# Expert outputs through rows in DRAM, and gate and up weights in runs of 4 KB, in a one-core encoder layer

## The chip, the cores and the metric

The kernel runs on one core of a Trainium2 chip. The metric is device time of one execution in microseconds (us). The core has TensorE (PE, with its weight loads PEld), VectorE (DVE), ScalarE (ACT), GpSimd (POOL) and SyncE (SP), which share an on-chip memory of 128 partitions (SBUF) and an accumulator memory (PSUM, 8 banks). 16 DMA engines move data between SBUF and DRAM; SP and POOL issue the DMAs here.

## The reference

One encoder layer on 512 tokens of width 1024, in float32: a mixer (a state space scan and a gated delta net), a cross attention over 256 memory rows, and a mixture of experts. Only the last part is touched. Each token goes to 2 of 32 experts, whose weights are 1024x256 (gate), 1024x256 (up) and 256x1024 (down):

```python
g_logits = (t @ wg).astype(F32) + bg.astype(F32)
p_top, g_idx = lax.top_k(jax.nn.softmax(g_logits, axis=-1), 1)
...
e_val, e_idx = lax.top_k(e_sel, MOE_TOPK)
e_w = jax.nn.softmax(e_val, axis=-1) * p_top
...
h = (jax.nn.silu(jnp.einsum('td,edf->tef', t, w_gate[sl]))
     * jnp.einsum('td,edf->tef', t, w_up[sl]))
h = h * combine[:, grp][..., None]
out = out + jnp.einsum('tef,efd->td', h, w_down[sl])
```

The result is added to the layer's input of this part and normalised. The weights of the 32 experts are 100.7 MB, 3.1 MB an expert.

## The kernel before, in words

The mixer and the cross attention fill the first 640 us. Then the routing (`moe_route`) works out for each expert up to 64 slots of tokens. Experts are worked on in 16 pairs of two, one on each half of the 128 rows of a tile. For pair q:

- `pair_tokens` (L1316): POOL gathers the slots' tokens from `t_scr` in DRAM by an indirect DMA (rows with a number past 511 are left out; 1,024 token slots in all, so 64 of the 128 rows of a pair on average) into one of two tiles `xg`; PE transposes them in 8 matmuls (L1327), ACT copies them to `xt`.
- `pair_up` (L1333): 16 matmuls of 512 columns (L1340) against the gate and up weights, then the gated product `hs` (ACT L1343, DVE L1344).
- `pair_down` (L1347): two transposes of `hs` (L1355), 8 matmuls of 512 columns (L1364) against the down weights into two banks; ACT and DVE write the result as a high and a low part `y`.
- `scatter` (L1370): a 0/1 matrix `st` of slots and tokens takes the slots back to the tokens' rows: for each of the 4 blocks of 128 tokens and 2 halves of the columns two matmuls (L1377; 16 a pair) and one DVE add into the residual `xr` (L1378).

The weights come in units of 1 MB, four of gate and up weights and two of down weights for a pair, 96 in all (`load_unit`, L1301). They have 19 places in SBUF that go round: 13 of gate and up weights, 6 of down weights, so some 3 pairs. SP issues each load when the matmuls that read the place before are done; a DMA also waits for the one eight before it in SP's queue. 18 units are loaded before the first pair starts, one more as soon as the first gather has landed, and 77 behind it. A gate or up unit is a tile `[P, 4, 2, 256]` in which gate and up columns take turns, so its two DMAs write runs of 256 numbers (1 KB), though the rows in DRAM hang together for 4 KB.

The order on each engine is fixed when the program is built, by a scheduler that follows estimated times; PE works on the matmuls of pair q+1, the down weights of pair q and the scatter of pair q-1 in turns. Banks 0 and 1 of PSUM serve both `pair_up` and `pair_down`. At the end (`moe_final`, L1380) each block is normalised and written out by SP.

Of the kernel before, what the change touches and what calls it, by code (L numbers as in the profile page):

```python
# [9 lines left out]
F32 = mybir.dt.float32  # L10
# [21 lines left out]
P = 128  # L32
# [11 lines left out]
def weave(*streams):  # L44
    """run generators side by side, (generator, number of its steps) each, evenly"""
    live = [[g, n, 0] for g, n in streams]
    while live:
        s = min(live, key=lambda t: (t[2] + 0.5) / t[1])
        s[2] += 1
        if next(s[0], s) is s:  # L50
            live.remove(s)
# [6 lines left out]
class Enc:  # L58
# [6 lines left out]
    def set_banks(self, **kw):  # L65
        """the PSUM banks of each stream of work: streams that run side by side do not share banks"""
        self.banks.update(kw)
        self.turn.update({n: 0 for n in kw})
# [7 lines left out]
    # ---------------------------------------------------------------- consts  # L76
    def consts(self):
# [13 lines left out]
        self.ltb = cp.tile([P, P], BF16, name="ltb")          # [t', t] = t' < t  # L91
# [14 lines left out]
    # ------------------------------------------------- normalise and transpose  # L106
    def rms_T(self, pool, tiles, gain, hi, lo, tag, between=None, junk=None):
        """tiles: list of [128 tok, D] token blocks -> hi/lo [128, 8, ntok] (feature p*8+k)."""
# [25 lines left out]
    # weight columns [128, 8, w]: staged, split into fp32r hi and lo parts  # L134
    def wsplit(self, src, w, lo_eng=None, tag="w"):
        """src: DRAM AP [128, 8, w]."""
# [9 lines left out]
    def mm3(self, ps, pairs, first=True, last=True):  # L146
        """pairs: list of ((lhsT_hi, lhsT_lo), (rhs_hi, rhs_lo))"""
# [6 lines left out]
    # ---------------------------------------------------------------- stage A  # L154
# [26 lines left out]
    def proj(self, c0):  # L181
        """feature-major projection of 128 columns from c0 -> PSUM [128, 512]"""
# [18 lines left out]
    # ---------------------------------------------------------------- S5  # L201
    def acc_exp(self, pool, out, x, n, tag):
        """out = exp(x) to float32 accuracy, x [128, n]"""
# [17 lines left out]
    def cmul(self, eng, pool, ore, oim, are, aim, bre, bim, shape, tag):  # L221
        """(ore + i oim) = a * b, elementwise on APs of the given shape"""
# [9 lines left out]
    def s5_params(self):  # L232
# [3 lines left out]
        with tc.tile_pool(name="s5t", bufs=1, side="right") as tq:  # L236
# [6 lines left out]
            with tc.tile_pool(name="s5i", bufs=1, side="right") as tp:  # L243
# [27 lines left out]
                # C^T: [lane, (re, -im), g, c']  # L271
# [5 lines left out]
                # step, a = exp(lam*step)  # L277
# [19 lines left out]
                # powers a^0 .. a^8  # L297
# [11 lines left out]
                # aR: conjugate of (fwd a^m, bwd a^(7-m));  aF: fwd a^(7-m), bwd a^m  # L309
# [6 lines left out]
                # a^8 with real part twice, (-im, im)  # L316
# [6 lines left out]
                # f = (a - 1)/lam  # L323
# [15 lines left out]
                # Bbar = f*b (a padded group at the end), B1 = a*Bbar  # L339
# [5 lines left out]
            with tc.tile_pool(name="s5l", bufs=1, side="right") as tl:  # L345
                # diag(d) per group
# [5 lines left out]
                for gg in range(8):  # L352
# [4 lines left out]
                    # P = aF * B1  # L357
# [3 lines left out]
                    # Ca_re, -Ca_im  # L361
# [5 lines left out]
                    # BcT: [(m c), cg, ri, (dir p)]  # L367
# [7 lines left out]
                    # local kernels  # L375
# [117 lines left out]
    # ---------------------------------------------------------------- GDN  # L493
# [23 lines left out]
    def gates(self):  # L517
# [6 lines left out]
        with tc.tile_pool(name="gt_", bufs=1) as tp:  # L524
# [5 lines left out]
            # rows 32i..: the projection's part from the feature blocks i and i + 4; the sums in token order  # L530
# [19 lines left out]
            # beta = 1/(1+exp(-x))  # L550
# [3 lines left out]
            # g = -exp(a_log) * softplus(a + dt)  # L554
# [17 lines left out]
            # chunk cumulative sums and totals  # L572
# [14 lines left out]
            # per-step scalars: rows of the forward chunk n, rows of the backward chunk 7-n  # L587
            # csr: -beta_f*egc_f | -egc_b ; csv: 1 | beta_b ; cso: egc_f | egc_b
# [13 lines left out]
    def gdn_alloc(self):  # L602
# [4 lines left out]
        self.kn = gp.tile([P, 4, 4, P], F32, name="kn")        # blk, h, d  # L607
        self.vc = gp.tile([P, 8, 4, P], F32, name="vc")        # step, h, dv
# [4 lines left out]
    def gdn_in(self, blocks, tp):  # L613
        """projection, convolution, silu, norms, token-major and feature-major operands.
        The transposes of a block come after the projections of the next ones."""
# [1111 lines left out]
```

## Time and profile before

| | us |
|---|---|
| runs | 959.79, 962.05, 950.4; median 959.79 |
| span of the profiled execution | 956.5 |
| experts, from the first gather (652.9) to the end | 303.6 |
| PE busy in the span | 842.3 (88%) |
| DVE, ACT, POOL busy | 548.9, 374.0, 274.6 |
| DMA | 173.25 MB, of it 161.30 MB read from and 15.17 MB written to DRAM |

The page gives the span of the profiled execution and no other time of it; the median of the runs lies 3.3 us above the span. A busy PE is not PE at its peak, as matmuls are pipelined. DMA shares can pass 1.0 because packets overlap in an engine.

### The profile page before, as it was taken

The numbers are of one execution on the slowest core, as the hardware profiler recorded it, in microseconds if no ns is written. First come the engines' busy times: TensorE is split into PE (matmuls) and PEld (weight loads), VectorE is DVE, ScalarE is ACT, GpSimd is POOL, SyncE is SP. The second block draws the span as 40 slices with busy tenths as digits, with TensorE's granted clock in tenths as the row PEclk, the third lists the DMA queues.
The fourth block names the chain that finished last, engine by engine and source line by source line (L and its number), as shares of the span: only waits on it lengthen the run. The fifth ranks groups of instructions, "written<-read, shape, count | busy, mean of one in ns | idle before, by whom it ended". The sixth has DMA issues, their size and how long they took to land.

```text
span 956.5 us, 14240 instructions
## 1 busy us (share of the span) xinstructions
PE 842.3 (88%) x5247; PEld 574.6 (60%) x5248; DVE 548.9 (57%) x1195; ACT 374.0 (39%) x815; POOL 274.6 (29%) x234
## 2 busy tenths in 40 slices
PE   5898888887855889898999999975999999999995
PEld 4676566666855757685788789972344344343432
DVE  5599999698999973235533634134144344344345
ACT  6544554675224328235524644322322122121224
POOL 3154597435542411003451332322100000000003
PEclk9997899999896898589999999996999999999998
DMA  8774223212531164317646325984999999999502
GB/s 203 135 92 130 79 87 94 73 56 78 163 108 58 49 120 116 64 45 209 216 144 198 111 66 189 360 288 134 342 379 364 365 377 362 366 375 363 199 1 90
DMA packets 173977, 173.25 MB, mean 181 GB/s; under 512 B 37584, under 2 KB 157392, under 8 KB 170064
## 3 DMA queue, kind: packets, MB, share of 16 engines
q1 hardware_dynamic: 171600, 168.11, 57.0%
q0 software_dynamic: 2304, 4.20, 1.3%
q8 instruction: 42, 0.69, 0.3%
q14 instruction: 31, 0.25, 0.1%
HBM read 161.30 MB, written 15.17 MB: 185 GB/s over the span
## 4 chain that ended last, share of the span: by engine, by line
PE 51%; DMA 4%; DVE 3%; ACT 3%; SPq 2%; issue 1%; POOL 0%; DVEq 0%; ACTq 0%; POOLq 0%
PE bank L1340 13%; PE bank L1364 7%; PE bank L1377 7%; PE bank L152 5%; PE bank L151 5%; PE bank L150 5%; PE bank L1327 2%; DMA tz<-w_scr 2%; DMA kvs<-kv_scr 1%; PE bank L850 1%; PE bank L833 1%; PE bank L802 1%; PE bank L1355 1%; PE bank L801 1%; SPq L430 1%
## 5 line engine op out<-in xcount | busy, mean ns | idle before, releaser
L1378 DVE TENSOR_TENSOR xr<-xr,bank 128x512 f32<-128x512 f32 x120 | 76.3, 683 | 117.8 <-PE bank L1377 117.6
L1340 PE MATMUL bank<-mw,xt 128*64 128x512 f32 x400 | 118.5, 609 | 0.0
L143 POOL TENSOR_TENSOR wlo<-wst,whi 128x1024 fp32r<-128x1024 f32 x24 | 58.3, 2433 | 56.5 <-ACT whi L142 39.2
L150 PE MATMUL bank<-htl,whi 128*128 128x512 f32 x160 | 68.0, 426 | 7.3 <-ACT whi L142 4.1
L1377 PE MATMUL bank<-y,st 128*128 128x512 f32 x240 | 70.2, 416 | 4.4 <-ACT y L1366 3.4
L1320 POOL DMA_INDIRECT xg<-t_scr,tidx x16 | 16.4, 1022 | 191.7 <-PE bank L1327 160.9
L1340 PEld LDWEIGHTS bank<-mw,xt 128*64 128x64 f32 x400 | 33.9, 139 | 59.6 <-issue 53.7
L152 PE MATMUL bank<-hth,wlo 128*128 128x512 f32 x160 | 66.5, 416 | 0.0
L151 PE MATMUL bank<-hth,whi 128*128 128x512 f32 x160 | 66.4, 415 | 0.0
L1343 ACT ACTIVATE hs<-bank,tw 128x256 f32<-128x256 f32 x16 | 7.6, 473 | 147.5 <-PE bank L1340 147.5
L1377 PEld LDWEIGHTS bank<-y,st 128*128 128x128 f32 x240 | 41.2, 189 | 38.7 <-issue 17.0
L973 POOL TENSOR_TENSOR wlo<-wst,whi 128x1024 fp32r<-128x1024 f32 x16 | 38.4, 2403 | 82.5 <-ACT whi L972 82.5
L142 ACT ACTIVATE whi<-wst 128x1024 fp32r<-128x1024 f32 x36 | 38.1, 1059 | 26.6 <-DMA wst<-in_w_in_dram 11.3
L641 DVE SCALAR_TENSOR_TENSOR cv<-xp,taps,cv 128x512 f32<-128x512 f32 x48 | 46.6, 972 | 0.4
L1364 PE MATMUL bank<-mw,hT 128*64 128x512 f32 x128 | 46.3, 601 | 0.0
L152 PE MATMUL bank<-mth,wlo 128*128 128x256 f32 x128 | 40.2, 314 | 6.7 <-POOL wlo L143 6.7
L150 PE MATMUL bank<-mtl,whi 128*128 128x256 f32 x128 | 40.4, 316 | 3.5 <-ACT zt L683 3.5
L1330 ACT ACTIVATE xt<-bank,gm 128x128 f32<-128x128 f32 x128 | 34.9, 386 | 20.6 <-PE bank L1327 20.3
L150 PEld LDWEIGHTS bank<-htl,whi 128*128 128x128 f32 x160 | 32.4, 203 | 15.3 <-ACT whi L142 4.4
L151 PE MATMUL bank<-mth,whi 128*128 128x256 f32 x128 | 39.5, 309 | 0.0
L152 PEld LDWEIGHTS bank<-hth,wlo 128*128 128x128 f32 x160 | 32.2, 201 | 7.6 <-issue 0.6
L150 PE MATMUL bank<-wlo,oh 128*128 128x256 f32 x128 | 36.7, 290 | 0.0
(552 smaller groups left out, 2236.3 us busy)
## 6 DMA issues: line engine op xcount, KB each, us to landing
mw<-in_moe_w_gate_dram SPq DMA_DIRECT2D x50, 512.0 KB, 10.0
mw<-in_moe_w_up_dram SPq DMA_DIRECT2D x50, 512.0 KB, 9.9
mw<-in_moe_w_down_dram SPq DMA_DIRECT2D x15, 1024.0 KB, 10.9
wst<-in_w_in_dram SPq DMA_DIRECT2D x20, 512.0 KB, 4.3
xl<-in_moe_w_down_dram SPq DMA_DIRECT2D x5, 1024.0 KB, 9.8
ol<-in_moe_w_down_dram SPq DMA_DIRECT2D x5, 1024.0 KB, 9.7
xh<-in_moe_w_down_dram SPq DMA_DIRECT2D x5, 1024.0 KB, 10.7
ca_scr<-ca SPq DMA_DIRECT2D x8, 512.0 KB, 2.7
```

Of the source, the lines that this page charges most:

```text
L142: nc.scalar.activation(hi, st, AF.Copy)
L143: (lo_eng or self.lo_eng).tensor_tensor(lo, st, hi.bitcast(F32), op=OP.subtract)
L150: self.nc.tensor.matmul(ps, ah, bl, start=(first and i == 0), stop=False)
L151: self.nc.tensor.matmul(ps, ah, bh, start=False, stop=False)
L152: self.nc.tensor.matmul(ps, al, bh, start=False, stop=(last and i == n - 1))
L641: v.scalar_tensor_tensor(cv, xp[:, w:w + T], taps[:, w, m:m + 1], cv, op0=OP.mult, op1=OP.add)
L973: nc.gpsimd.tensor_tensor(lo, st, hi.bitcast(F32), op=OP.subtract)
L1330: nc.scalar.activation(xt[:, k], ps[:, (k % 4) * P:(k % 4 + 1) * P], AF.Copy, scale=self.gm[:, k:k + 1])
L1340: nc.tensor.matmul(pg[w * 64:w * 64 + 64], xt[:, k, w * 64:w * 64 + 64], un[k // 4 * 2 + w][:, k % 4].rearrange("p a n -> p (a n)"), start ...
L1364: nc.tensor.matmul(py[w * 64:w * 64 + 64], hT[:, k, w * 64:w * 64 + 64], wd[w][:, k, c], start=(k == 0), stop=(k == 1))
L1377: nc.tensor.matmul(po, st[:, b * P:(b + 1) * P], y[:, w, c], start=(i == w == 0), stop=(2 * i + w == n - 1))
L1378: nc.vector.tensor_tensor(xs[b][:, c], xs[b][:, c], po, op=OP.add)
```

## The change

The gate and up tile becomes `[P, 2, 4, 256]`: gate first, then up, each in runs of 1024 numbers; the matmul reads its 512 columns as two runs of 256. Pairs 0 to 13 no longer use `scatter`: `pair_store` writes the pair's output as plain float32 (one half by ACT, one by DVE) to a tile `yd` (two of them), and POOL sends its rows by an indirect DMA to `y_scr`, a DRAM tensor of two rows for each token (first and second expert; the row number `didx` is a new column of the routing's table). SP fills `y_scr` with zeros first, 4.2 MB, from the zeroed `xg[1]`. Behind the last weights SP reads the 4.2 MB of `y_scr` back into four tiles `yb`; POOL adds the two rows of a token, DVE adds the sum to the residual. Pairs 14 and 15 keep `pair_down` and `scatter`.

```diff
-        av = rp.tile([P, 2, 4, 8, 32], BF16, name="av")
+        av = rp.tile([P, 2, 4, 9, 32], BF16, name="av")
...
+        for j in range(2):
+            g_.tensor_scalar(av[:, j, :, 8], aj[:, j], 512.0 * j, None, op0=OP.mult)
...
-            slots(32, slice(2, 8))
+            slots(32, slice(2, 9))
+
+            v.tensor_tensor(self.didx, self.tfl, pi[:, 128:144], op=OP.add)
...
-        t = pool.tile([P, 4, 2, 256], F32, name=tag, tag=tag)
+        t = pool.tile([P, 2, 4, 256], F32, name=tag, tag=tag)
         k = slice(j // 2 * 4, j // 2 * 4 + 4)
         for i, n in enumerate(('moe_w_gate', 'moe_w_up')):
-            self.dma(t[:, :, i], A[n][0, e].rearrange("(p k) n -> p k n", k=8)[:, k])
+            self.dma(t[:, i], A[n][0, e].rearrange("(p k) n -> p k n", k=8)[:, k])
...
-                nc.tensor.matmul(pg[w * 64:w * 64 + 64], xt[:, k, w * 64:w * 64 + 64], un[k // 4 * 2 + w][:, k % 4].rearrange("p a n -> p (a n)"),
-                                 start=(k == 0), stop=(k == 7))
+                nc.tensor.matmul(pg[w * 64:w * 64 + 64].rearrange("p (a n) -> p a n", a=2), xt[:, k, w * 64:w * 64 + 64],
+                                 un[k // 4 * 2 + w][:, :, k % 4], start=(k == 0), stop=(k == 7))
...
+    def pair_store(self, q, hs, wd, wk, chunks):
...
+        y = wk.tile([P, D], F32, name="yd")
+        for i, c in enumerate(slice(*c) for c in chunks):
+            py = self.ps("y")[:, :c.stop - c.start]
+            for k in range(2):
+                for w in range(2):
+                    nc.tensor.matmul(py[w * 64:w * 64 + 64], hT[:, k, w * 64:w * 64 + 64], wd[w][:, k, c],
+                                     start=(k == 0), stop=(k == 1))
+            if i:
+                nc.vector.tensor_copy(y[:, c], py)
+            else:
+                nc.scalar.activation(y[:, c], py, AF.Copy)
+        nc.gpsimd.indirect_dma_start(out=self.y_scr, out_offset=bass.IndirectOffsetOnAxis(ap=self.didx[:, q:q + 1], axis=0),
+                                     in_=y, in_offset=None, bounds_check=2 * T - 1, oob_is_err=False)
...
-        for t in xg:
+        for t in xg[::-1]:
             nc.gpsimd.memset(t, 0.0)
+        nc.sync.dma_start(self.y_scr.rearrange("(p r) n -> p r n", p=P), xg[1][:, None, :].to_broadcast([P, 8, D]))
...
-                    ys = [self.pair_down(q - 1, hs[q - 1], [un[6 * q - 2 + j] for j in range(2)], wk, chunks)]
+                    wd = [un[6 * q - 2 + j] for j in range(2)]
                     if q < 15:
-                        for c in chunks:
-                            for b in range(4):
-                                self.scatter(xs, ys, b, slice(*c))
+                        self.pair_store(q - 1, hs[q - 1], wd, wk, chunks)
+                    else:
+                        for b, t in enumerate(yb):
+                            nc.gpsimd.tensor_tensor(t[:, 0], t[:, 0], t[:, 1], op=OP.add)
+                            nc.vector.tensor_tensor(xs[b], xs[b], t[:, 0], op=OP.add)
+                        pool, tag = place(0, 71)
+                        ys = [self.pair_down(q - 1, hs[q - 1], wd, wk, chunks, pool.tile([P, 2, D], F32R, name="yprev", tag=tag))]
+                    if q == 14:
+                        yb = []
+                        for b in range(4):
+                            pool, tag = place(0, 67 + b)
+                            t = pool.tile([P, 2, D], F32, name="yb", tag=tag)
+                            for j in range(2):
+                                nc.sync.dma_start(t[:, j], self.y_scr[j * T + b * P:j * T + (b + 1) * P])
+                            yb.append(t)
```

The order of the instructions moves in three places. On PE, in the middle of the experts: before, the matmuls of `pair_up` (L1340) and those against the down weights (L1364) are broken up by the scatter (L1377).

```order
L1340 MATMUL bank_6847<-mw_8_6534,xt 64x512
L1377 MATMUL bank_6823<-y,st 128x512 x2
L1377 MATMUL bank_6827<-y,st 128x512 x2
L1377 MATMUL bank_6831<-y,st 128x512 x2
L1340 MATMUL bank_6847<-mw_9_6537,xt 64x512
```

Now the 16 matmuls of `pair_up` (L1344) stand together, as do groups of four against the down weights (L1385); L1331 is the transposes of the gathered tokens, L1377 now those of `hs`.

```order
L1344 MATMUL bank_6799<-mw_1_6588,xt 64x512
L1331 MATMUL bank_6914<-ident,xg_6153 128x128 x4
L1331 MATMUL bank_6923<-ident,xg_6153 128x128 x4
L1385 MATMUL bank_6865<-ol_6637,hT 64x512
L1385 MATMUL bank_6865<-xh_6639,hT 64x512
L1385 MATMUL bank_6865<-ol_6637,hT 64x512
L1385 MATMUL bank_6865<-xh_6639,hT 64x512
L1377 MATMUL bank_6932<-ident,hs 128x128 x2
L1331 MATMUL bank_6993<-ident,xg_6154 128x128 x4
```

What moved: nothing stands between the matmuls of one product any more. On POOL, which before had nothing but the gathers there, the stores stand between them (from the seventh gather on, of sixteen), and the last six behind the last gather:

```order
L1391 DMA y_scr<-yd,didx 1024x1024 x2
L1324 DMA xg_6153<-t_scr,tidx 128x1024
L1324 DMA xg_6154<-t_scr,tidx 128x1024
L1391 DMA y_scr<-yd,didx 1024x1024
L1324 DMA xg_6153<-t_scr,tidx 128x1024
L1324 DMA xg_6154<-t_scr,tidx 128x1024
L1391 DMA y_scr<-yd,didx 1024x1024
```

Each store also waits for the store before it to be complete, as both write `y_scr`, and holds up what stands behind it on POOL meanwhile. On SP, the end of the loads: the down weights of pairs 14 (`ol`, `xh`) and 15 (`xl`, `mw_0`), the norm's gain, then the eight reads of `y_scr`, which wait for all the stores.

```order
L1318 DMA oh_7299<-in_moe_w_up_dram 128x1024
L1318 DMA ol_7345<-in_moe_w_down_dram 128x2048
L1318 DMA xh_7347<-in_moe_w_down_dram 128x2048
L1318 DMA xl_7412<-in_moe_w_down_dram 128x2x512
L1318 DMA mw_0_7413<-in_moe_w_down_dram 128x2x512
L1318 DMA xl_7412<-in_moe_w_down_dram 128x2x512
L1318 DMA mw_0_7413<-in_moe_w_down_dram 128x2x512
L1721 DMA gF<-in_norm_final_dram 128x1024
L1707 DMA yb<-y_scr 128x1024 x8
L1422 DMA out_dram<-fo 128x1024 x4
```

Before, the outputs stood right behind the gain; the order of the weights among themselves is as it was. On PE the store of pair 13 depends on four matmuls against its down weights that stand behind 15 of the 16 matmuls of `pair_up` of pair 15.

## Rows read from the trace of the kernel before

**Rows 1.** The page: its first line and, of the 40 equal slices of the span (23.9 us each), the busy share of the 16 DMA engines in tenths, and the GB/s they moved.

```profile
span 956.5 us, 14240 instructions
...
DMA  8774223212531164317646325984999999999502
GB/s 203 135 92 130 79 87 94 73 56 78 163 108 58 49 120 116 64 45 209 216 144 198 111 66 189 360 288 134 342 379 364 365 377 362 366 375 363 199 1 90
```

**Rows 2.** Busy time by stretch: the stretch in us and its length, then busy us (and instructions) of PE, PEld, DVE, ACT, POOL, and at the end granted clock, DMA share and GB/s.

```profile
640.00:655.00 15.00, 2.52 (x41) 2.08 (x40) 12.28 (x64) 1.11 (x4) 7.31 (x11) 0.60 0.20 77
655.00:665.00 10.00, 8.20 (x40) 3.75 (x40) 1.39 (x4) 2.17 (x8) 1.65 (x2) 0.58 0.71 206
665.00:675.00 10.00, 10.00 (x50) 3.88 (x48) 0.48 (x1) 4.77 (x13) 0.99 (x1) 1.00 0.88 265
...
680.00:880.00 200.00, 195.47 (x836) 82.88 (x838) 81.06 (x135) 45.93 (x137) 10.99 (x12) 1.00 1.07 368
880.00:893.00 13.00, 13.00 (x54) 5.11 (x55) 4.42 (x8) 2.64 (x9) 0.00 (x0) 1.00 0.81 295
893.00:897.00 4.00, 4.00 (x16) 1.24 (x13) 1.73 (x4) 0.82 (x2) 0.00 (x0) 1.00 0.00 0
```

**Rows 3.** The waits of PE from 659 to 945 us, all of them: engine and what waited, <- what it waited for, us in total, times, longest.

```profile
PE bank L1377 <- ACT y L1366: 3.4, 5, 0.7
PE bank L1377 <- DVE y L1367: 1.0, 4, 0.3
PE bank L1327 <- ACT xt L1330: 0.7, 1, 0.7
```

**Rows 4.** PE's timeline at the first pair and among the last ones: start in us, length in us, line, what is written<-read, shapes, count of records, and the idle time before with its releaser.

```profile
657.65 1.97 PE L1327 MATMUL bank<-ident,xg 128*128 128x128 f32 x8 [1.40 <-DMA xg<-t_scr,tidx]
659.55 1.98 PE L1340 MATMUL bank<-mw,xt 128*64 128x512 f32 x4
...
901.51 1.66 PE L1377 MATMUL bank<-y,st 128*128 128x512 f32 x6
903.10 3.65 PE L1340 MATMUL bank<-mw,xt 128*64 128x512 f32 x14
...
907.73 1.06 PE L1327 MATMUL bank<-ident,xg 128*128 128x128 f32 x8
...
917.34 3.65 PE L1340 MATMUL bank<-mw,xt 128*64 128x512 f32 x16
920.92 0.50 PE L1355 MATMUL bank<-ident,hs 128*128 128x128 f32 x2
```

**Rows 5.** The end of the chain of waits that ended last: start, us, what.

```profile
937.06 1.87 PE bank L1364 x8
938.93 6.15 PE bank L1377 x26
```

**Rows 6.** Three short stretches, columns as in rows 2: in the first the input x lands (four DMAs of 512 KB in rows of 4 KB), in the second gate and up weights and a gather, in the third down weights.

```profile
3.50:8.00 4.50, 0.32 (x2) 0.32 (x3) 1.30 (x6) 2.78 (x5) 0.79 (x2) 1.00 1.01 404
788.50:796.00 7.50, 7.50 (x40) 3.09 (x36) 2.11 (x4) 1.07 (x3) 0.99 (x1) 1.00 1.09 352
...
783.00:787.00 4.00, 4.00 (x17) 1.19 (x16) 1.83 (x4) 1.74 (x7) 0.00 (x0) 1.00 1.02 411
```

**Rows 7.** DMA in the stretch from 680 to 880 us: packets by size, and the queue of the gathers (packets, MB, share of the 16 engines' time).

```profile
DMA packets 52877, 73.68 MB, mean 368 GB/s; under 512 B 2842, under 2 KB 49359, under 8 KB 50051
...
q0 software_dynamic: 1728, 2.84, 4.1%
```

**Rows 8.** SP's queue: start, us, line, what is loaded.

```profile
665.10 0.37 SPq L1314 DMA_DIRECT2D mw<-in_moe_w_gate_dram  x1
...
881.78 0.38 SPq L1314 DMA_DIRECT2D xh<-in_moe_w_down_dram  x1
896.73 0.57 SPq L1314 DMA_DIRECT2D xl<-in_moe_w_down_dram  x1
...
899.44 1.01 SPq L1683 DMA_DIRECT2D gF<-in_norm_final_dram  x1
```

**Rows 9.** POOL's timeline in the routing: start, us, line, what, and the idle time before with its releaser.

```profile
641.38 1.86 POOL L1642 MEMSET xg<- 128x1024 f32 x2 [1.66 <-PE bank L1129]
...
650.03 0.91 POOL L1284 TENSOR_TENSOR sl<-asg,e 128x256 f32<-128x256 f32 x1
652.85 1.27 POOL L1320 DMA_INDIRECT xg<-t_scr,tidx  x1 [1.92 <-DVE slot L1287]
```

**Rows 10.** DMA issues by line over the whole span: out<-in, queue, count, KB each, median us from issue to landing.

```profile
out_dram<-fo SPq DMA_DIRECT2D x4, 512.0 KB, 2.7
...
xg<-t_scr,tidx POOLq DMA_INDIRECT x16, 6.7
```

**Rows 11.** Two groups by shape: sums of two 128x1024 tiles on POOL and on DVE, busy us and mean ns of one.

```profile
L143 POOL TENSOR_TENSOR wlo<-wst,whi 128x1024 fp32r<-128x1024 f32 x24 | 58.3, 2433 | 56.5 <-ACT whi L142 39.2 <-PE bank L267 11.4 <-DVE rt L415 5.9
L143 DVE TENSOR_TENSOR wlo<-wst,whi 128x1024 fp32r<-128x1024 f32 x12 | 17.6, 1468 | 3.3 <-ACT whi L142 3.3
```

**Rows 12.** The last steps of all engines: the last add into xr, a product of the norm, and the output.

```profile
945.10 0.69 DVE L1378 TENSOR_TENSOR xr<-xr,bank 128x512 f32<-128x512 f32 x1
...
945.87 1.76 POOL L1392 TENSOR_TENSOR fo<-xr,gF 128x512 f32<-128x512 f32 x1
...
946.57 4.00 SPq L1398 DMA_DIRECT2D out_dram<-fo  x4
```

More of the change, by code (lines that the diff above doesn't have):

```diff
@@ L1345, in pair_up, with pair_down @@
         return hs
-    def pair_down(self, q, hs, wd, wk, chunks, y=None):
+    def pair_down(self, q, hs, wd, wk, chunks, y):
         nc = self.nc
@@ L1357, in pair_down @@
         nc.scalar.activation(hT.rearrange("p k t -> p (k t)"), ph[:, :256], AF.Copy)
-        if y is None:
-            y = wk.tile([P, 2, D], F32R, name="y", bufs=1)
         for c in (slice(*c) for c in chunks):
@@ L1368, in pair_down @@
         return st, y
+    def pair_store(self, q, hs, wd, wk, chunks):
+        nc = self.nc
+        ph = self.ps("hp")
+        for k in range(2):
+            nc.tensor.transpose(ph[:, k * P:(k + 1) * P], hs.rearrange("t (p k) -> t k p", k=2)[:, k, :], self.ident)
+        hT = wk.tile([P, 2, P], F32, name="hT")
+        nc.scalar.activation(hT.rearrange("p k t -> p (k t)"), ph[:, :256], AF.Copy)
+        y = wk.tile([P, D], F32, name="yd")
+        for i, c in enumerate(slice(*c) for c in chunks):
+            py = self.ps("y")[:, :c.stop - c.start]
+            for k in range(2):
+                for w in range(2):
[7 more added lines that the diff above has]
+                                     in_=y, in_offset=None, bounds_check=2 * T - 1, oob_is_err=False)
     def scatter(self, xs, pairs, b, c):
@@ L1498, in build @@
         self.t_scr = scr("t_scr", (T, D))
+        self.y_scr = scr("y_scr", (2 * T, D))
         self.sidx = scr("sidx", (32 * T, 1), I32)
@@ L1601, in build @@
         for n, shape, dt in (("wt", [P, 2, 4], F32), ("slot", [P, 2, 4], I32), ("nblk", [1, 32], I32), ("cmax", [1, 1], I32),
-                             ("tidx", [P, 16], I32), ("tfl", [P, 16], F32), ("tw", [P, 2, 16], F32)):
+                             ("tidx", [P, 16], I32), ("didx", [P, 16], I32), ("tfl", [P, 16], F32), ("tw", [P, 2, 16], F32)):
             setattr(self, n, mcp.tile(shape, dt, name=n))
```

## The prediction, made before the changed kernel ran

> **What bounds the kernel now.** I read the page's slices first: from 670 us on (slice 29) the DMA engines are busy all the time at 360 to 380 GB/s, for nine slices, and then stop while the kernel goes on for two and a half more [rows 1]. The table by stretch puts numbers to it [rows 2]: from 680 to 880 us DMA moves 368 GB/s at a share over 1, and in the same stretch PE is busy 195.5 of 200 us at the full clock. From 893 to 897 DMA moves nothing, and PE is busy without a gap. So two resources run side by side at nearly the same pace, and the one that ends last decides. That is PE: its waits come to 5.1 us in all from 659 to 945, none of them for a DMA [rows 3], and the chain of waits ends in PE's scatter [rows 5]. From SP's queue: the continuous stream of weights begins at 665.1 and its last load is issued at 881.8; the last four loads, the down weights of pair 15 in halves, come at 896.7, when a place is free [rows 8]. PE works on the experts from 659.55 [rows 4] to 945.1 [rows 5], 17.8 us a pair.
>
> **Part 1, the scatter goes.** Six scatter matmuls hold PE from 901.51 to 903.10, 0.265 us each [rows 4]. 14 pairs by 16 are 224 matmuls, 59 us of PE. What stays in a pair: `pair_up` 2 x 3.65, its eight token transposes 1.06, the `hs` transposes 0.50 [rows 4], the down product 2 x 1.87 [rows 5]: 12.6 us. Since the matmuls of one product now stand together, I take these unbroken lengths. 16 pairs are 202 us, and PE alone could be done with them at 659.5 + 202 + 2 (the first 16 records of `pair_up` took 5.53, at a granted clock of 0.58 [rows 2, 4]) = 863. All 59 us would come off only if DMA let them. It doesn't: DMA is late next. DVE also loses 112 adds and ACT and DVE some copies; neither limits, at 81 and 46 busy us in 200 [rows 2], so nothing for that.
>
> **Part 2, runs of 4 KB.** Nearly all packets of the stage are under 2 KB, the runs of 1 KB of the gate and up units [rows 7]. While those land DMA moves 352 GB/s at a share of 1.09; while down weights land, in runs of 8 KB, 411 GB/s at 1.02. The input x, in rows of 4 KB, came in at 404 [rows 6]. So the rate hangs on the run, and gate and up units should go from 352 to 404: a unit of 1.0486 MB from 2.98 to 2.60 us. The ends are 352 (nothing gained) and 411; I take 404 because x has the same run. The matmul reads two runs of 256 columns instead of one of 512; no row shows that, it could cost PE nothing up to a few per cent, and PE has 20 us to spare, so nothing.
>
> Here a page stands against the change: the Trainium skill, "DMA: Bandwidth & Descriptors", Bandwidth, says that between DRAM and SBUF a limit of about 358 GB/s for a core binds. The trace disagrees, with 404 and 411 held for 4 to 5 us. By the page the 88 MB still to move behind 665 us would take some 246 us as an estimate, and the time would come to 945.
>
> **Part 3, the traffic added.** Each store moves the rows that the gather of its pair brought: 64 of 128 on average, 0.26 MB. Twelve gathers took 4.1% of 200 us of the 16 engines [rows 7], 0.7 us each; a store has the same rows and bytes the other way, so 0.7 us. The ends: 0.65 us at 404 GB/s, and 6.7 us if the engines did nothing else from a store's issue until it had landed, taking a gather's median [rows 10]. I take the value of the gather, which is nearest in every respect. The zero fill, 4.2 MB, can be issued when the first memset is done (641.38 + half of 1.86) and takes 10.5 us at x's rate, to 653; from 640 to 655 DMA moves only 77 GB/s [rows 2], so the cover is there; the first gather is issued at 652.85 [rows 9] and may share the engines' last us with it. I take 0.5 us (0 to 3). The second gather waits until the fill has read `xg[1]`; its tokens are needed at 665. The two new POOL products in the routing are near 0.4 us each; one falls into an idle gap and the other pushes the next product, of 0.91 us [rows 9], by as much; DVE now needs that product a little later, so nothing for it. On POOL's queue a store waits for its `yd` and for the store before; the gather behind it is wanted by PE only a pair later, and a landing takes 6.7 us [rows 10] against 17 a pair: hidden.
>
> **The sum.** First the model on the kernel before. Behind 665.1 stand 51 gate and up units, 24 down units before the last two, and 13 gathers: 51 x 2.98 + 24 x 2.56 (at 411) + 13 x 0.7 = 222.5. From 665 to 675 DMA ran at 265 instead of 352 [rows 2], 2.5 us lost while the first places come free. 665.1 + 225 = 890; DMA did stop between 880 and 893. Now: 51 x 2.60 = 132.5, 26 x 2.56 = 66.5 (the last two no longer wait, since PE is ahead), gathers 9, 13 stores 9, start 3.5, fill 0.5: 221. The last weight lands at T = 886. PE, at 863, is ahead, and follows the weights from about pair 12 on.
>
> Then the tail, which is new. The last gate and up unit lands four down units before T, at T - 10.2. Half a `pair_up` (3.65) and the four matmuls of pair 13 behind it (1.9) and the copy (0.7): T - 4. Store 13: 6.7 from issue to landing, T + 2.7. Only then may SP read `y_scr`: 4.2 MB at 404 are 10.4 us and 1.4 to land (2.7 for an output DMA less its 1.3 of transfer [rows 10]): T + 14.5. POOL adds the last two rows (2.43), DVE adds to the residual (1.47) [rows 11], then a product and the two scatter adds of the last block (2.1): T + 20.5. In the kernel before 10.7 us lie between the last add (945.10 + 0.69 [rows 12]) and the end; one block is left here, so 10. The scatter of pairs 14 and 15 lies beside the readback: from T on 3.7 us of matmuls and 6.2 [rows 5]. The span ends at T + 30.5 = 916.5, 40 us less than 956.5. What lies around the span I take from the median, 959.8 - 956.5 = 3.3: **920 us**, 4% less. Of the 59 us of PE and the 20 of DMA, half comes through, because the work that PE did behind the stream is replaced by a readback behind the stream.
>
> **The rivals.**
> - *The runs bring nothing.* The gate and up units stay at 2.98: T = 906, time 940. For it: 404 was seen for 4.5 us only, early in the kernel. Against it: 411 for each pair of down units in the middle of the stage [rows 6]. 0.10. (The page's limit would act in this direction.)
> - *Stores and readback cost more.* At 2.5 us of the engines a store, between my ends, T is 23 later: 943; only past 5.2 us does it become 2% slower. For it: nothing in the trace writes single rows by an index. Against it: the same rows gathered cost 0.7. 0.09.
> - *Less tail.* Store 13 lands sooner, or the rate is nearer 411: 905 to 909. 0.09.
> - *Slower: PE falls to the low clock.* Where PE waits for weights it may drop to 1.2 GHz, as it did in the routing (0.60 from 640 to 655, PE busy 2.5 of 15 us [rows 2]). A pair then takes 25 us instead of 12.6. DMA gives a pair in 17 (4 x 2.60 + 2 x 2.56 + 1.4), so it begins to matter when a third of PE's time is at the low level, and makes the kernel over 2% slower from some 45% on: 16 pairs of 18.3 us end at 952, and 24 us of tail bring the span to 976. Against it: PE has no gap until pair 12; and from 665 on, after a few us of unbroken work, the clock was at 1.00 [rows 2], so a slow PE, which has no gaps, speeds up again. The Trainium skill, "TensorE: Matmul & The Clock Gate", HAM oscillation, describes such a kernel, in which each group of matmuls waits for its weights and starts at the low clock; the trace has not yet such a stretch. 0.05.
>
> **How the numbers follow.** The forecast, 909 to 931, has 0.67: its ends are a fill, a start and a tail that are some us off, and gate and up rates of 390 to 411. A measurement of this kernel tells about 2% from no change, that is 19 us: faster is under 940.6, slower over 979. Faster: 0.67 + 0.09 + 0.08 of the 0.19 of the first two rivals, which lie about that line = 0.84. Slower: 0.05. The same: the other 0.11. The range from 905 to 944 takes in the forecast, the runs without gain and most of the dearer stores; left out are the slow clock and the far ends.
>
> **What would show it.** In the changed kernel: packets under 2 KB gone from the stage; 400 GB/s or more while gate and up weights land (352 would make part 2 wrong); PE waiting for DMA of weights from about pair 12, not before; the last weight at 886, some 5 us earlier than before; the reads of `y_scr` issued some 3 us behind it, and 27 us from there to the end. If DMA stands still between loads, or PE waits for a gather behind a store, the order on POOL or SP is what I have misjudged; if PE's clock is under 0.9 from 680 on, the last rival holds.

## The result and the profile after

Four runs of the changed kernel took 929.45, 917.63, 930.29 and 917.18 us, median 923.5; the kernel before, on the same chip, 960.1. The ratio is 0.963, interval 0.955 to 0.972: 3.7% faster. The profiled execution is that of 929.45 us.

The runs of one kernel spread over some 10 us, most of which arises long before the experts: in the fourteen traces here the first load of weights behind the gather (SP, `xl<-in_moe_w_gate_dram`) is issued at 657.7 to 659.1 us where TensorE's granted clock between 400 and 500 us was 0.88 or 0.89, and at 646.3 to 650.9 where it was 0.97 or 0.98. So below I also give a trace's **stage**, from that load to the end of the span. Busy time by stretch (columns as in [rows 2]) of two executions of the changed kernel, with stages of 927.3 - 658.1 = 269.2 and 914.5 - 646.3 = 268.2; a difference of 1 us between two stages is therefore read as none:

```profile
400.00:500.00 100.00, 96.81 (x524) 73.23 (x522) 45.39 (x79) 42.55 (x75) 33.38 (x33) 0.88 0.46 148
```

```profile
400.00:500.00 100.00, 96.70 (x559) 74.44 (x556) 47.98 (x82) 42.69 (x76) 34.09 (x31) 0.98 0.46 147
```

The kernel before has 956.5 - 657.7 = 298.8. The page of after, to be held against [rows 1]:

```profile
span 927.3 us, 13626 instructions
...
PEclk9998798999896787959899999998799999898896
DMA  8855222222451207611763623597799999999952
GB/s 205 140 86 123 94 92 71 84 60 70 120 168 53 76 18 137 137 46 47 234 215 114 245 96 121 183 405 290 269 394 409 414 412 406 404 406 403 410 223 116
```

The plateau is at 403 to 414 GB/s instead of 362 to 379, and two slices with less follow, in which the readback lies. By stretch, against [rows 2]:

```profile
640.00:655.00 15.00, 2.82 (x44) 2.38 (x43) 12.12 (x62) 1.22 (x4) 7.78 (x13) 0.58 0.91 362
...
680.00:880.00 200.00, 169.59 (x756) 68.87 (x758) 14.67 (x25) 45.41 (x145) 24.32 (x25) 0.94 1.02 409
880.00:885.00 5.00, 5.00 (x26) 1.62 (x24) 0.48 (x1) 0.47 (x1) 0.00 (x0) 1.00 0.73 279
885.00:893.00 8.00, 7.37 (x34) 2.65 (x32) 1.17 (x2) 1.22 (x3) 0.98 (x1) 1.00 0.16 60
893.00:905.00 12.00, 11.79 (x49) 5.55 (x46) 5.64 (x8) 3.80 (x8) 5.50 (x3) 1.00 0.86 334
905.00:927.00 22.00, 2.58 (x11) 1.47 (x9) 15.19 (x21) 6.89 (x16) 14.94 (x10) 0.66 0.27 106
```

The zero fill shows in the first line (77 GB/s before). PE is no longer full, and the stream of weights thins out at about 885 (the last load, issued at 876.4, has landed in full at 889). The readback is the line from 893 on. In the last one PE is done and DVE and POOL share 22 us. DMA from 680 to 880 us, as in [rows 7]: the packets under 2 KB have gone from 49359 to 3937.

```profile
DMA packets 21098, 81.78 MB, mean 409 GB/s; under 512 B 3937, under 2 KB 3937, under 8 KB 18039
...
q0 software_dynamic: 3600, 6.46, 8.5%
```

PE's longest waits from 659 us on (columns as in [rows 3], where no DMA appeared):

```profile
PE bank L1385 <- DMA mw<-in_moe_w_down_dram: 9.3, 5, 4.3
PE bank L1385 <- DMA ol<-in_moe_w_down_dram: 5.5, 1, 5.5
PE bank L1385 <- DMA xl<-in_moe_w_down_dram: 4.6, 1, 4.6
```

The tail, from the timeline (columns as in [rows 4]):

```profile
867.79 1.94 PE L1385 MATMUL bank<-mw,hT 128*64 128x512 f32 x2 [4.27 <-DMA mw<-in_moe_w_down_dram]
870.64 2.82 PE L1385 MATMUL bank<-mw,hT 128*64 128x512 f32 x5 [0.92 <-DMA mw<-in_moe_w_down_dram]
873.26 11.55 PE L1344 MATMUL bank<-mw,xt 128*64 128x512 f32 x49
887.23 1.88 PE L1385 MATMUL bank<-mw,hT 128*64 128x512 f32 x8
890.60 0.98 POOL L1391 DMA_INDIRECT y_scr<-yd,didx  x1 [24.87 <-ACT hs L1347]
893.53 4.58 SPq L1707 DMA_DIRECT2D yb<-y_scr  x8
...
898.65 2.35 POOL L1697 TENSOR_TENSOR yb<-yb 128x1024 f32<-128x1024 f32 x1 [7.07 <-PE bank L1366]
901.85 2.66 POOL L1697 TENSOR_TENSOR yb<-yb 128x1024 f32<-128x1024 f32 x1 [0.85 <-DMA yb<-y_scr]
902.78 1.36 DVE L1402 TENSOR_TENSOR xr<-xr,bank 128x512 f32<-128x512 f32 x2
904.46 1.29 POOL L1416 TENSOR_TENSOR fo<-xr,gF 128x512 f32<-128x512 f32 x1
904.54 2.30 DVE L1698 TENSOR_TENSOR xr<-xr,yb 128x1024 f32<-128x1024 f32 x1 [0.40 <-POOL yb L1697]
905.72 3.35 POOL L1697 TENSOR_TENSOR yb<-yb 128x1024 f32<-128x1024 f32 x1
909.02 1.27 POOL L1416 TENSOR_TENSOR fo<-xr,gF 128x512 f32<-128x512 f32 x1
910.61 1.22 DVE L1698 TENSOR_TENSOR xr<-xr,yb 128x1024 f32<-128x1024 f32 x1
910.81 3.23 POOL L1697 TENSOR_TENSOR yb<-yb 128x1024 f32<-128x1024 f32 x1
914.83 1.22 DVE L1698 TENSOR_TENSOR xr<-xr,yb 128x1024 f32<-128x1024 f32 x1
914.98 2.19 POOL L1416 TENSOR_TENSOR fo<-xr,gF 128x512 f32<-128x512 f32 x1
```

Half of pair 13's down product runs from 867.8 on, held up by its weights. The other half stands behind the up products of pairs 14 and 15 (`L1344`; 62 of their 64 records lie ahead of it, 49 of them in the row shown) at 887.2, so store 13 goes at 890.6 and the eight reads at 893.5. DMA's rate falls at about 905; the last read, issued at 897.2, has landed 10.0 us later, at 907.2. The last of POOL's sums ends at 914.0, 6.9 us after that. Here L1697 is POOL's sum of two rows of tokens, L1698 VectorE's add of it, L1402 a scatter add and L1416 POOL's product of the final norm.

### The profile page after: what moved, and what is told of

Its sections match the earlier page's. It is cut to its first block, busy times and chain, and to the rows that moved or that the text cites. A ratio compares the mean times of both kernels' runs of the same rounds, so it can differ in the third digit from the quotient of the medians.

```text
span 927.3 us, 13626 instructions
## 1 busy us (share of the span) xinstructions
PE 781.3 (84%) x5023; PEld 547.1 (59%) x5024; DVE 471.9 (51%) x1060; ACT 367.2 (40%) x801; POOL 302.0 (33%) x254
## 5 line engine op out<-in xcount | busy, mean ns | idle before, releaser
L1344 PE MATMUL bank<-mw,xt 128*64 128x512 f32 x400 | 114.1, 609 | 1.7 <-ACT yd L1390 1.3
L1348 DVE SCALAR_TENSOR_TENSOR hs<-hs,tw,bank 128x256 f32<-128x256 f32 x16 | 7.7, 480 | 173.1 <-ACT hs L1347 173.1
L1344 PEld LDWEIGHTS bank<-mw,xt 128*64 128x64 f32 x400 | 38.5, 143 | 55.9 <-issue 49.9
L1385 PE MATMUL bank<-mw,hT 128*64 128x512 f32 x120 | 45.7, 664 | 10.9 <-DMA mw<-in_moe_w_down_dram 9.3
L1324 POOL DMA_INDIRECT xg<-t_scr,tidx x16 | 16.4, 1024 | 115.7 <-PE bank L1331 101.4
L1391 POOL DMA_INDIRECT y_scr<-yd,didx x14 | 14.0, 1001 | 93.5 <-ACT yd L1390 25.0
L151 PEld LDWEIGHTS bank<-hth,whi 128*128 128x128 f32 x160 | 33.0, 206 | 6.7 <-issue 0.2
## 6 DMA issues: line engine op xcount, KB each, us to landing
mw<-in_moe_w_up_dram SPq DMA_DIRECT2D x50, 512.0 KB, 12.6
xh<-in_moe_w_down_dram SPq DMA_DIRECT2D x5, 1024.0 KB, 13.3
```

Of the source, the lines that this page charges most:

```text
L151: self.nc.tensor.matmul(ps, ah, bh, start=False, stop=False)
L1324: self.gather = g_.indirect_dma_start(out=xg, out_offset=None, in_=self.t_scr, in_offset=bass.IndirectOffsetOnAxis(ap=self.tidx[:, q:q + 1 ...
L1344: nc.tensor.matmul(pg[w * 64:w * 64 + 64].rearrange("p (a n) -> p a n", a=2), xt[:, k, w * 64:w * 64 + 64], un[k // 4 * 2 + w][:, :, k % 4 ...
L1385: nc.tensor.matmul(py[w * 64:w * 64 + 64], hT[:, k, w * 64:w * 64 + 64], wd[w][:, k, c], start=(k == 0), stop=(k == 1))
L1391: nc.gpsimd.indirect_dma_start(out=self.y_scr, out_offset=bass.IndirectOffsetOnAxis(ap=self.didx[:, q:q + 1], axis=0), in_=y, in_offset=No ...
```

## The experiments

**1. The parts of the change, one at a time.** x1 is the kernel before with the 4 KB runs alone, the edit below reversed; x2 the changed kernel with

```diff
-        t = pool.tile([P, 2, 4, 256], F32, name=tag, tag=tag)
+        t = pool.tile([P, 4, 2, 256], F32, name=tag, tag=tag)
```

and the matching slices in the loads and in `pair_up`.

> The kernel before with nothing but the 4 KB runs. Theory (the runs are worth time only once TensorE is lighter): the stream moves 404 GB/s instead of 352 while TensorE lets it, but the 224 scatter matmuls still make a pair 12.6 us or more on TensorE, which sets the end: 950 to 960 us, as before; the weights land earlier or the queue waits for free places. Rival (the runs carry the gain by themselves): about 25 us faster, 930 to 940 us.

Measured: 950.5 us, ratio 0.997 (0.992 to 1.002), stage 299.1 against 298.8: no change. (The kernel before had a median of 958.5 beside it; the two medians differ within the spread told above.) x1 by stretch:

```profile
680.00:720.00 40.00, 40.00 (x178) 16.89 (x176) 14.50 (x24) 8.03 (x24) 2.97 (x3) 1.00 1.02 409
...
860.00:880.00 20.00, 19.06 (x78) 7.75 (x77) 10.23 (x18) 1.95 (x4) 0.00 (x0) 1.00 0.66 256
```

DMA starts at 409, runs out of free places and falls to 256, while PE stays full: from 660 to 945 SP waits 100.3 us for `pair_up` (L1340) to free a place, where it waited 16.7 before. The theory holds, the rival (930 to 940) is out.

> The changed kernel with the gate and up weights back in 1 KB runs. Theory (the weight stream bounds the stage once the scatters are gone): 352 GB/s instead of 409 from 658 to 885 us, so the last weight lands 20 to 30 us later, at 905 to 915, and the time is 943 to 950 us, 20 to 25 us above the changed kernel. Rival (TensorE carries the gain, the runs are idle gain): 924 us, no different from the changed kernel.

Measured: 942.8 us, ratio 0.987 (0.983 to 0.991), stage 290.3. x2 by stretch:

```profile
680.00:880.00 200.00, 160.00 (x723) 66.84 (x722) 15.07 (x26) 45.49 (x147) 24.19 (x24) 0.92 1.06 366
880.00:905.00 25.00, 15.79 (x54) 4.67 (x56) 0.48 (x1) 1.47 (x3) 0.97 (x1) 0.73 1.04 379
```

366 GB/s, and the stream thins out at about 909. The theory holds, with a median 0.2 us under its range; the rival (924) is out. Of the 29.6 us of stage that both parts save, the stores alone bring 8.5, the runs alone nothing, and the runs on top of the stores 290.3 - 269.2 = 21.1.

**2. The price of the stores.** x3 leaves out

```diff
-        nc.gpsimd.indirect_dma_start(out=self.y_scr, out_offset=bass.IndirectOffsetOnAxis(ap=self.didx[:, q:q + 1], axis=0),
-                                     in_=y, in_offset=None, bounds_check=2 * T - 1, oob_is_err=False)
```

> The changed kernel without its 14 indirect stores (the output leaves out what the experts of pairs 0 to 13 add; the reads at the end bring back the zeros of the fill). Theory: each store costs the weight stream its bytes (0.7 us each, so the last weight about 9 us earlier), the y tiles come free without waiting for a landing, and the reads at the end need not wait for the store of pair 13 (about 5 us): 908 to 914 us. Rival (the stores ride along for nothing, and only the wait for the last one counts): 918 to 920 us, last weight where it is, 885.

Measured: 912.0 us, ratio 0.952 (0.947 to 0.958), stage 252.6: 16.6 us less. Here reads of the rows go in the middle of the last weights:

```profile
871.60 0.54 SPq L1318 DMA_DIRECT2D mw<-in_moe_w_down_dram  x1
872.94 0.34 SPq L1719 DMA_DIRECT2D gF<-in_norm_final_dram  x1
874.21 4.22 SPq L1705 DMA_DIRECT2D yb<-y_scr  x4
```

Four of the eight reads were issued at 860.3 already, ahead of the last four loads of weights. The stream, weights and all reads, thins out at about 886, where the changed kernel has the weights alone. 4.2 MB of reads are 10 us at 409: so the 14 stores cost DMA about 10 us, an estimate, as theirs is the only traffic that is gone. The other 6 of the 16.6 us are what is left for the wait of the reads for store 13 (8.5 us from 885 to 893.5 in the changed kernel); no run takes this wait away alone. The median lies in the theory's range, and the rival is out; the last weight's own landing tells nothing here, as half of the reads go ahead of it.

**3. Who adds the rows.** x4: two adds per block on VectorE, no sum on GpSimd.

```diff
-                            nc.gpsimd.tensor_tensor(t[:, 0], t[:, 0], t[:, 1], op=OP.add)
                             nc.vector.tensor_tensor(xs[b], xs[b], t[:, 0], op=OP.add)
+                            nc.vector.tensor_tensor(xs[b], xs[b], t[:, 1], op=OP.add)
```

> The changed kernel with both rows of a token added to x by VectorE (two adds a block), and no sum on GpSimd. Theory (the last 20 us are set by the chain of GpSimd's four sums, 2.4 to 3.4 us each, slowed by VectorE working beside them): four sums and a late last add go, eight adds of 1.2 us on VectorE come: 4 to 6 us faster, 918 to 920 us. Rival (the reads of the rows, done at 905 us, and VectorE set the end): 923 to 925 us, no change.

Measured: 925.9 us, ratio 0.968 (0.963 to 0.973), stage 266.1. The median shows no gain, and the stage is 2 to 3 us shorter than the two of the changed kernel (268.2 and 269.2): less than the theory's 4 to 6, and more than the rival's nothing. GpSimd's sums are not the only thing that sets the end.

**4. Store 13 early.** x5 writes pair 13's down product ahead of `pair_up` of pair 14, and leaves it out at its old place (those lines aren't shown); x6 is the same with x4's adds; x0 repeats the changed kernel beside them.

```diff
             for q in range(16):
+                if q == 14:
+                    self.pair_store(13, hs[13], [un[82 + j] for j in range(2)], wk, chunks)
                 hs[q] = self.pair_up(q, xt[q], [un[6 * q + j] for j in range(4)], wa)
```

> The changed kernel as it is, for the comparison with the two runs beside it on the same chip. Every theory: 917 to 930 us, and the stage from the first weight load behind the gather to the end 269 us, as in its first trace (927.3 - 658.1).

> The changed kernel with pair 13's down product and store written ahead of pair 14's up product instead of behind it, so that TensorE computes both its halves one after the other before the up products of pairs 14 and 15. Theory (store 13 waits 17 us for a half of that product that stands behind two up products, and the eight reads wait for the store): store 13 goes at 874 to 878 us instead of 890.6, the reads are in at 895 to 898 instead of 905, and the stage takes 260 to 263 us instead of 269; median 914 to 918. Rival (the end is set by TensorE's last products and the final norm whatever the reads do): the reads come earlier, and the stage still takes 267 to 270 us.

> The kernel with store 13 early and, besides, both rows of a token added by VectorE and none by GpSimd. Theory: with the rows in earlier, GpSimd's four sums (2.4 to 3.4 us each) no longer stand behind the reads, so that their removal brings 0 to 3 us more: 258 to 262 us of stage. Rival (VectorE, which then has eight adds of 1.2 to 1.9 us between the final norm's steps, becomes the end): as long as with the sums or up to 3 us longer, 261 to 266.

Measured: x0 923.8 us (ratio 0.965, 0.959 to 0.970), stage 268.2. x5 930.5 (0.972, 0.966 to 0.977), stage 274.8; x6 931.3 (0.969), 272.2. Store 13 did go early, 219.5 us into the stage instead of 232.5, and the kernel was no faster: stages 4 to 6.6 us longer than x0's. x5's DVE, and PE behind it:

```profile
888.78 1.22 DVE L1700 TENSOR_TENSOR xr<-xr,yb 128x1024 f32<-128x1024 f32 x1 [19.14 <-POOL yb L1699]
892.24 3.35 DVE L1700 TENSOR_TENSOR xr<-xr,yb 128x1024 f32<-128x1024 f32 x1 [2.23 <-POOL yb L1699]
895.51 0.86 DVE L1348 SCALAR_TENSOR_TENSOR hs<-hs,tw,bank 128x256 f32<-128x256 f32 x2
```

```profile
896.03 0.70 PE L1359 MATMUL bank<-ident,hs 128*128 128x128 f32 x2 [13.38 <-DVE hs L1348]
```

The scheduler, presumably because it expected the rows sooner, had put two adds ahead of the scaling of the hidden layers of pairs 14 and 15 (`hs`). VectorE sat in front of them and TensorE waited 13.4 us. Neither the theories nor the rivals had this. The reads were in 242.9 us into the stage, 5 earlier than in x0 (248.0), though the store went 13 earlier: now they stand in the DMA queue with the last weights.

**5. The adds tied behind the products.** x7 is x5 with the four adds moved behind the last subtraction of pair 15's down product; x8 with both rows on VectorE.

```diff
+            with tc.issue_after(self.y_last.ins):
+                for b, t in enumerate(yb):
+                    nc.gpsimd.tensor_tensor(t[:, 0], t[:, 0], t[:, 1], op=OP.add)
+                    nc.vector.tensor_tensor(xs[b], xs[b], t[:, 0], op=OP.add)
```

> Store 13 early, as in the run before it, with the four adds of the rows read back tied behind the last subtraction of pair 15's down product on VectorE. Theory (in that run two adds stood ahead of the scaling of pairs 14 and 15's hidden layers on VectorE, and TensorE waited 13.4 us for it; the earlier reads themselves were a gain): store at 220 us of the stage, reads in at 241, the last subtraction at 243, GpSimd's sums done at 247 to 249, VectorE's adds and the final norm behind them, end at 260 to 263 us of the stage, against 268 of the changed kernel; median 915 to 919. Rival (the adds of a block must run beside TensorE's products; all of them behind the last subtraction cost what the earlier reads gain): 266 to 270 us, median 922 to 925.

> The same with both rows of a token added by VectorE, none by GpSimd. Theory: eight adds of 1.2 us from 243 us of the stage, done at 253, against sums on GpSimd to 247 to 249 and an add of 1.2 behind the last: 2 to 4 us longer than the run before it, 262 to 267 us. Rival (GpSimd and VectorE slow one another, so that the sums and adds side by side take longer than the adds alone): 1 to 3 us shorter than the run before it.

Measured: x7 920.2 us (0.960, 0.956 to 0.965), stage 265.8; x8 919.1 (0.960, 0.955 to 0.964), 268.9. x7's stage is 2 to 3 us shorter than the changed kernel's, not 7, and its rival's range (266 to 270) is the nearer one. The store goes 220.3 us into the stage and the reads are in at 243.2, 5 us earlier, and part of that is lost again: four adds in a row hold up the scatter adds, and with them PE's banks. x7's next scatter:

```profile
909.80 1.22 PE L1401 MATMUL bank<-yprev,st 128*128 128x512 f32 x2 [4.98 <-DVE xr L1402]
```

x8's theory holds for the difference by the stage (3.1 us more than x7), not for the level; the medians do not part the two.

**6. An order written out.** x9: up product of 14, down product of 13 in banks of its own, up product of 15 on PE; on VectorE each block's add directly ahead of its two scatter adds. (The lines that take the adds from their old place aren't shown.)

```diff
+                with tc.issue_after(self.dn_last.ins) if q == 15 else contextlib.nullcontext():
+                    hs[q] = self.pair_up(q, xt[q], [un[6 * q + j] for j in range(4)], wa)
...
+                        self.set_banks(y=(3, 4))
+                        with tc.issue_after(self.up_last.ins):
+                            self.pair_store(q - 1, hs[q - 1], wd, wk, chunks)
...
+                with tc.issue_after(self.v_last.ins):
+                    nc.gpsimd.tensor_tensor(yb[b][:, 0], yb[b][:, 0], yb[b][:, 1], op=OP.add)
+                    nc.vector.tensor_tensor(xs[b], xs[b], yb[b][:, 0], op=OP.add)
```

x10: the same with both rows on VectorE. x11: the second row of a token added by TensorE into the scatter's bank, and the first by VectorE as in x10,

```diff
+        nc.tensor.matmul(po, self.ident, row[:, c], start=False, stop=True)
```

> The changed kernel with an order written out for the last three pairs: on TensorE pair 14's up product (whose weights are there) ahead of pair 13's down product, that with both halves together in banks of its own, pair 15's up product behind it; on VectorE the add of a block's rows directly ahead of that block's two scatter adds, instead of all four in a row. Theory (what is left of the tail is queue order: 5 us of TensorE idle ahead of pair 13's down product, a store that goes 17 us late, adds in bulk ahead of the scatter adds): store 13 at 217 to 220 us of the stage, reads in by 237 to 240, TensorE's last product 243 to 246 instead of 249, the end at 254 to 259 us of the stage against 268; median 908 to 914. Rival (behind the reads 22 to 25 us remain whatever the order, as in the runs so far): 262 to 266, median 917 to 921.

> The same order with both rows of a block added by VectorE and none by GpSimd. Theory: GpSimd's four sums (2.4 us alone) no longer stand ahead of its four products of the final norm, VectorE has four more adds of 1.2 us: within 2 us of the run before it, either way. Rival (sums and adds side by side slow one another by half, as the 3.2 to 3.4 us of three of the sums in the changed kernel suggest): 3 to 5 us shorter.

> The written-out order, with the first row of a token added by VectorE and the second by TensorE, as a product with the identity into the scatter's own PSUM bank (8 products more, 0.45 to 0.64 us each by the rows of other 128x512 float32 products). Theory (what ends last is VectorE's queue: in the run before it, VectorE was busy for 9.97 of the 10 us behind the last products): four adds of 1.2 us leave it, TensorE has about 4 us more in a stretch in which it waits: 257 to 260 us of the stage against 262.2 in the run before it; median 914 to 920. Rival (TensorE's eight products, in front of the adds that read their banks, stand in the same chain): 261 to 265 us.

Measured: x9 925.2 us (0.967), stage 269.0; x10 922.7 (0.966, 0.962 to 0.971), 262.2; x11 913.0 (0.957, 0.951 to 0.963), **260.4**. x9's theory fell, and its rival (262 to 266) too: PE began pair 15's scatter 238.2 us into the stage, 3.4 earlier than in x0, but then waited for VectorE and ended it at 250, as there. DVE (9.02 of 10 us) and POOL (10.00) were full. Busy time by stretch of x9, then x10, then x11:

```profile
890.00:900.00 10.00, 3.80 (x14) 2.10 (x12) 9.02 (x9) 2.68 (x8) 10.00 (x5) 0.91 0.06 23
```

```profile
890.00:900.00 10.00, 1.85 (x4) 0.97 (x4) 9.97 (x14) 3.90 (x10) 3.70 (x4) 0.55 0.16 62
```

```profile
890.00:900.00 10.00, 8.63 (x28) 4.90 (x26) 9.57 (x16) 4.07 (x12) 3.73 (x4) 1.00 0.16 65
```

And x9's timeline:

```profile
889.59 1.23 DVE L1737 TENSOR_TENSOR xr<-xr,yb 128x1024 f32<-128x1024 f32 x1 [1.52 <-POOL yb L1736]
889.71 8.96 POOL L1736 TENSOR_TENSOR yb<-yb 128x1024 f32<-128x1024 f32 x3 [0.16 <-issue]
...
893.08 3.36 DVE L1737 TENSOR_TENSOR xr<-xr,yb 128x1024 f32<-128x1024 f32 x1 [0.88 <-POOL yb L1736]
```

An add of 1.22 us takes 3.36 where it begins behind GpSimd's sums; the one at 889.59, which began just ahead of them, took its 1.23. Without the sums (x10) the same order is 6.8 us shorter by the stage, more than the 3 to 5 of that run's rival, and its theory (within 2) fell. (The rival spoke of three slow sums in the changed kernel; there are two, of 3.35 and 3.23.) x10 takes away the sums' own time as well as the holding up, and no run parts the two. With half the adds on TensorE (x11) the stage is 1.8 us shorter still, little more than two traces of one kernel differ by, and just outside the 257 to 260 of its theory. x11 has the lowest median of all complete kernels, 10.9 us under x0's (7.8 by the stage); but the intervals of the two ratios still touch (0.951 to 0.963, 0.959 to 0.970), so that the runs alone do not yet show the gain.

## Why the prediction was right, and where not

920 was forecast, 923.5 measured, inside the forecast's own range. In the span of the profiled execution 916.5 was worked out and 927.3 measured: the sum is 10.8 us short. That the median came within 3.5 is in part luck: the traces from which 956.5 and 927.3 come both have the lower clock between 400 and 500 us (0.89 and 0.88), and half of the four runs in the median are some 12 us shorter. What lies around the span is 2.1 us (929.45 - 927.3), not the 3.3 that I took from a median and the trace of another execution.

- *The scatter goes, DMA is late next.* Right: PE has 169.6 busy us in 200 where it had 195.5, and waits for weights. It does so from 766.9 on, in the down product of pair 7, not 12, and for down weights alone. Up to there PE took 13.2 us a pair rather than 12.6 (from 684.4 to 763.8, six pairs, at a granted clock of 1.00 from 680 to 760), with 6.6 us of short waits for ACT and VectorE, which the sum had at nothing; that cost nothing, since DMA sets the pace.
- *Runs of 4 KB, 352 to 404.* Right: 409 over 200 us, gate, up and down units mixed. x1 and x2 show both halves of the argument: worth nothing under the scatter, 21 us without it. The matmul that reads two runs of 256 columns showed no price: 16 of its records take 3.65 us as before. The rival without gain, and the page's limit beside it, are out: the Trainium skill's "DMA: Bandwidth & Descriptors", Bandwidth, names some 358 GB/s for DRAM to SBUF and says elsewhere in that section that this is the share with a pair's other core streaming too. Here one core runs, at 409.
- *A store 0.7 us.* Right: the share of the indirect queue rose from 4.1 to 8.5% of 200 us by 13 stores' packets, 0.68 us each; x3 gives about 10 us for 14, by a difference.
- *Fill 0.5 us.* Within its bounds: the first gather went at 653.51 instead of 652.85 [rows 9], 0.66 later, of which 0.3 is a later start of the routing (the memset at 641.67, not 641.38) and the rest a wait for VectorE's routing, not for the fill; the second waited 1.17 us for the fill, and PE did not wait for its tokens.
- *T = 886.* Right for the stream, which thins out at about 885; the last load of weights had landed in full at 889, and nothing waited for it.
- *Store 13 landed at T + 2.7.* Wrong by 4.8: the reads went at 893.5, not 888.7. Two errors partly cancel in this. The store was issued at 890.6 and not at T - 4 = 882, 8.6 later: I had taken both halves of pair 13's down product to follow half a `pair_up`, and on PE one half stands behind nearly two whole ones. And it landed in 2.7 us instead of 6.7, where the median of all 14 stores is 8.0; DMA was nearly idle then (60 GB/s from 885 to 893). x5 and x7 show that the store can go 12 to 13 us earlier and that the reads then come 5 earlier; with the adds tied behind the products (x7) 2 to 3 us of that reach the end.
- *Reads done 11.8 us after issue.* 1.8 short: 13.6, from 893.5 to the last landing at 907.2.
- *16.0 us from the reads to the end.* Wrong by 4.1: 20.1. I had let the first three blocks be finished beside the reads, so that the last block's sum of 2.43 follows them at once. In fact POOL's sums alternate with its products of the norm, and sums and VectorE's adds hold one another up; the fourth sum began 3.6 us after the last landing, took 3.23, and ended 6.9 us after it, 4.4 more than the sum had. Behind that sum 13.3 us follow, where I had 1.47 + 2.1 + 10 = 13.6: this part was right. So the step that failed is the queue ahead of the last block, not the last block. In the changed kernel's order x4 gives back 2 to 3 us of it; in the written-out order x10 gives 6.8.
- *The low clock.* Out as a rival: 0.94 from 680 to 880. It fell to 0.83 from 860 to 880, where PE waited 4.3 us for weights, and was 1.00 from 880 to 905, where PE was busy for 24.2 of 25 us. There it cost a little on the way to store 13: at 870.64 five records against the down weights took 2.82 us, where eight took 1.88 at 887.23, some 1.5 us by these rows (an estimate).

## What to carry to other kernels

Two resources at the same pace have to be relieved together: one part of this change was worth nothing alone and 21 us with the other, so a part that measures as no change need not be dropped. Work taken off the busy engine and put behind the stream as a transfer leaves a new tail; price it by the queue of every engine that adds the results, in the order in which the queues stand, not by one block. And a step moved earlier can make the scheduler move its consumers earlier too, ahead of work that others wait for: tie them.

## What the runs showed of the hardware that I had not expected

GpSimd and VectorE hold one another up on some operands only. In the changed kernel two scatter adds with one input in PSUM took 1.36 us, 0.68 each, at 902.78 in the middle of a sum on GpSimd, as long as without one (0.69, [rows 12]). With both inputs of the add in SBUF, the one of the two engines that began second paid. The add at 904.54 began just behind a GpSimd product (904.46 to 905.75) and took 2.30 instead of 1.22. The adds at 910.61 and 914.83 began just ahead of a GpSimd sum (910.81) and a product (914.98) and took their 1.22, while the sum took 3.23 instead of 2.35 and the product 2.19 instead of 1.27. The Trainium skill, "SBUF — State Buffer", Who interferes with whom, says which operands these are: a VectorE instruction with two SBUF inputs contends with a GpSimd instruction that reads SBUF, and one with at most one SBUF input, outside some faster modes, doesn't. The rows agree. x11 goes the way that follows from this: the second row comes into the scatter's PSUM bank by a product with the identity, so that four adds with two SBUF inputs are gone, for eight products more on an engine that was busy for 1.85 of 10 us there in x10.
